# A hybrid diffusion step on one core: score products over all array rows, keys and queries in one transfer each

## The chip, the core and the metric

The kernel runs on one core of a Trainium2 chip. The core has a matrix engine (TensorE, PE in the rows; its weight loads are PEld), a vector engine (DVE), an activation engine (ACT), a general engine (POOL) and a queue engine that issues transfers (SP). Transfers between main memory and the on-chip memory run on 16 DMA engines that the core owns. The on-chip memory has 128 partitions. Each engine works through its own instruction list in order and waits on semaphores.

The metric is device time in microseconds (us) of one execution. Before the change three runs took 2118.08, 2121.22 and 2123.41 us, a median of 2121.22 us.

## The reference

One inference step for a context group (256 tokens) and a latent group (1024 tokens) that share their weights. Layer 0 mixes with attention and with an RWKV-7 scan side by side, layer 1 with gated linear attention (GLA). Cut to what matters here:

```python
def block_attention(q, k, v):                      # 8 query heads, 2 key/value heads, head size 64
    s = jnp.einsum('bqkgd,bskd->bkgqs', qi, k).astype(jnp.float32) * scale
    p = jax.nn.softmax(s, axis=-1)
    return jnp.einsum('bkgqs,bskd->bqkgd', p, v)

def even_mixer(h, ...):                            # layer 0
    qa, ka, va, ga, zb, gb = split_cols(h @ w_in, EV_SPLITS)
    q, k, v = rms_norm(qa), rms_norm(ka), va       # latent: rotary on q and k, cached keys in front
    o_a = block_attention(q, keys, vals) * silu(ga)
    zb = token_shift(zb, shift_mu)
    # RWKV-7, forward and backward: s = s*w + (s@-kk)(kk*a) + v k ; y = s@r
    o_b = (group_norm(y) + bonus) * silu(gb)
    return concatenate([o_a, o_b]) @ w_out

m = silu(cond) @ mod_w[i] + mod_b[i]               # shift, scale, gate of each layer
x = x + gate * mixer(rms_norm(x) * (1 + scale) + shift)
```

Latent queries attend to 512 cached, 1024 latent and no other keys; context queries to the 256 context keys.

## The kernel before, in words

**One list scheduler writes the order.** The kernel is written as many generators (tasks) that ask for buffers by a tag and record instructions. A class `Sched` holds a cost for each instruction (`_instr`), estimates when each engine is free and each buffer ready, and again and again issues the recorded instruction that could start first (`drive`). So the static order on every engine follows from these costs and from conditions between tasks (`sch.until`). All instructions are recorded by one helper, so nearly all rows of the profile name its line, L354 (L356 after the change). Groups are told apart by the names of their tiles. Compute instructions keep the scheduler's order. Transfers, all on SP's queue, keep their own order, which the framework makes and in which a transfer can stand earlier.

**Layer 0.** Tokens lie on the free axis (groups of 256, 512 and 512 tokens), channels on the partitions. Projections split numbers into a high and a low part (`hhi`, `hlo`, `whi`, `wlo`) and make three products. First come RWKV's inputs, the queries, keys and values and the eight gate units (`gated_unit`; the last ones write `gb`). Queries and keys are written to main memory as a high and a low part (`qh`, `kh`).

**The change of rooms.** When the layer's units are issued (`flags["left"] == 0`), `room_attn` closes the right half of the on-chip memory and opens attention's tiles there. When the eighth gate unit is over and `room_attn` is done, `room_rwkv` closes the left half (`hhi`, `hlo`, the weights) and opens RWKV's tiles, with masks to load and constants to fill (`LL`, `Z`, `ring`, `UV`, mostly on POOL and ACT). Then three kinds of work run side by side until about 1310 us: 40 RWKV segments (`rwkv_seg`, tiles `AR`, `BK`, `Vs`), twelve attention units, and the modulation products of the later layers (`mods`).

**Scores.** For each key/value head v the tile `KA[v]` holds the high parts of 64 channels in partitions 0 to 63 and the low parts in 64 to 127; `KB[v]` holds the high parts again and a row of ones in partition 64. For a query head `QA` holds the queries' high parts twice, and `QB` their low parts and in row 64 the negated maxima. `maxima` makes approximate scores with one product over `QA` and `KA` and reduces them on DVE (tile `mx`); the negated maxima (`mr`) go to `QB`'s row 64 by a small transfer. `attend` then makes the exact scores in two products, and ACT takes the exponential:

```python
PE.matmul(p[:, 0:n], lhsT=KA[kv][:, kc], rhs=Q[hh][0][:, 0:n], start=True, stop=False)
PE.matmul(p[:, 0:n], lhsT=KB[kv][0:65, kc], rhs=Q[hh][1][0:65, 0:n], start=False, stop=True)
```

There are 208 such pairs. `KA[v]` is filled by two transfers of 64 partitions, `QA` by two, `KB[v]` and `QB` by one each. There are four buffers of `QA` and of `QB`, so the queries of the next units are loaded while earlier ones are used.

**Modulation.** `mod_cols` loads 1 MB of `mod_w` into a buffer `mw` (in this stage there is one, so a load waits until the products of the one before have read it) and makes eight products that use 32 columns of the array each.

Of the kernel before, what the change touches and what calls it, by code (L numbers as in the profile page):

```python
# [22 lines left out]
NK = DM // P  # L23
# [80 lines left out]
class Sched:  # L104
# [71 lines left out]
    def _instr(self, name, op, f, a, k):  # L176
# [19 lines left out]
        if name == "pe":  # L196
            lhs = pattern(k.get("lhsT", a[1] if len(a) > 1 else None))
            m = 1
            for d in lhs.shape[1:]:
                m *= d  # L200
            rows = lhs.shape[0]
            turned = op == "transpose" or k.get("is_transpose")

            if turned:
                cost = max(2 * n / 2300, m / 1170)
            elif lhs.dtype == F32:
                cost = 2 * max(2 * n / 2300, m / 1170)
            elif lhs.dtype == F32R:
                cost = max(n / 2300, m / 1170)
            else:  # L210
                cost = max(n, 64) / 2300
            cost = 1.06 * cost + 0.0025
            size = lambda x: 32 if x <= 32 else 64 if x <= 64 else P
            late = (size(rows), size(m), lhs.start_partition() // 32, out.start_partition() // 32)
        elif name == "dve":
            srcs = [x for _, x in aps if x is not out]
            psum = any(x.tensor.space == PSUM for x in [out] + srcs)
            if op == "reduce_max":
                n = 1
                for d in srcs[0].shape[1:]:  # L220
                    n *= d
            wide = n
            if not psum and (op in ("tensor_copy", "tensor_scalar") or all(x.dtype == F16 for x in [out] + srcs)):
                wide = n / 2
            cost = (62 if psum else 66) / 960 + wide / 960
            if op == "reciprocal":
                cost = (62 + n * 6) / 960
            if op == "tensor_tensor_scan":
                cost += n / 960
            if out.shape[0] <= 64 and not n == 1:  # L230
                cost += 0.11
            late = not psum and op != "reduce_max"
            if op in ("tensor_scalar", "scalar_tensor_tensor"):
                cost += (0.0, 0.057, 0.09)[sum(1 for x in srcs if x.shape[1:] == [1] or tuple(x.shape[1:]) == (1,))] if n > 1 else 0.0
        elif name == "act":
            psum = any(x.tensor.space == PSUM for _, x in aps)
            cost = (0.051 if psum else 0.094) + n * 0.833e-3
            if n > 1:
                cost += (0.0, 0.05, 0.17)[min(2, sum(1 for q, x in aps if q in ("scale", "bias", 2)))]
            if out.shape[0] <= 64 and n > 1:  # L240
                cost += 0.11
        elif name == "pool":
            if op == "tensor_tensor":
                cost = 0.15 + n * (1.66e-3 if any(0 == d[0] for _, x in aps for d in x.ap[1:]) else 2.1e-3)
                if k.get("op", a[-1]) == ALU.pow:
                    cost = 0.56
            elif op == "memset":
                cost = 0.14 + n * 0.42e-3
            else:
                cost = 0.16 + n * (0.833e-3 if len(aps) == 2 else 1.5e-3)  # L250
            late = op != "memset"
        else:
            cost, late = 0.47, n * out.shape[0] * 4 / 270e3
        return f, a, k, name, cost, late, reads, writes, slots

    def _choice(self, slot, taken=()):
# [227 lines left out]
def tile_hybrid_dit_step(ctx: ExitStack, tc: tile.TileContext, I, C, O):  # L484
# [63 lines left out]
    def mod_cols(i, c0, n, bank, row, ready=lambda: True):  # L548
# [15 lines left out]
                b = yield from get(row, False)  # L564
                D.dma_start(out=b[0:2, 0:n], in_=I["mod_b"][i:i + 1, c0:c0 + n].to_broadcast([2, n]))
        yield from sch.until(ready)
        for a in range(2):
            with sch.together():
                for s in range(4):
                    k = 4 * a + s  # L570
                    PE.matmul(p[32 * s:32 * s + 32, :], lhsT=sT[:, k, :], rhs=ws[k // nk][:, k % nk, :], start=(a == 0), stop=(a == 1))
            for x in ws[4 * a // nk:4 * (a + 1) // nk]:
                put("mw", x)
        m4 = yield from get("m4", False)
        m = m4[:, 0:n]
        copy(m, p)
# [123 lines left out]
    vt_d = [dram.tile([T, P], F32, name=f"vt{p}") for p in range(4)]  # L700
    bv_d = [dram.tile([P, T], F32, name=f"bv{p}") for p in range(4)]
    kh_d = dram.tile([P, 2, PAST + T], F32, name="kh")
    vo_d = dram.tile([P, 14, P], F32, name="vo")
    ga_d = [dram.tile([P, T], F32, name=f"ga{p}") for p in range(4)]
    gb_d = [dram.tile([P, T], F32, name=f"gb{p}") for p in range(4)]
# [7 lines left out]
    get, put = sch.get, sch.put  # L713
    el = cst.tile([P, 2, 4, 20], F32, name="el")
    left, right = (ctx.enter_context(ExitStack()) for i in range(2))
    flags = dict(left=0, gates=0, attn=False, keys=False, rwkv=False, mods=False, normed=False, gla=False, gl=False, units=0)

    def pool(stack, name, **k):
        return stack.enter_context(tc.tile_pool(name=name, bufs=1, reuse_waits="tile", **k))
# [18 lines left out]
    def layer0():  # L738
# [44 lines left out]

        def gated(col, dst):

            def use(g, t0, n, p):
                t1 = yield from get("gt", False)
                S.activation(out=t1[:, 0:n], in_=p, func=AF.Tanh, scale=0.5)
                V.scalar_tensor_tensor(out=t1[:, 0:n], in0=t1[:, 0:n], scalar=1.0, in1=p, op0=ALU.add, op1=ALU.mult)
# [8 lines left out]
        def gated_unit(i, col, dst):  # L798
            yield from sch.until(lambda: flags["left"] <= GATES[i])
            yield from gated(col, dst)  # L800

            def done():
                flags["gates"] += 1
            sch.then(done)

        def gates():
            for i in range(8):
# [379 lines left out]
    def room_attn():  # L1187
# [11 lines left out]
        sT = ac.tile([P, NK, 32], F32, name="sT1")  # L1199
        for x in ("QA", "QB"):  # L1200
            slots(x, 4, [P, 512], F32R)
        slots("mx", 2, [P, 4, 4])
        slots("mr", 1, [4, P], F32R)
        slots("rcp", 1, [P, 512])
# [3 lines left out]
        yield from move("a", "po", 1)  # L1208
        yield from move("a", "b", 3)
        yield from move("pj", "b", 2)  # L1210
        for x in range(2):
            load_keys(0, x)
        for v in range(2):
            V.memset(KB[v][64:65, :].bitcast(F32), 1.0)
        D.dma_start(out=sT.rearrange("p k c -> p (k c)"), in_=sT_d)
        V.memset(ones64, 1.0)

# [3 lines left out]

    def load_keys(v, x):

        D.dma_start(out=(KA, KA, KB)[x][v][64 * (x % 2):64 * (x % 2) + 64, :].bitcast(F32), in_=kh_d[64 * v:64 * v + 64, x % 2, :])

    def keys():

        yield from sch.until(lambda: flags["attn"])
        for v, x in ((0, 2), (1, 0), (1, 1), (1, 2)):
            load_keys(v, x)  # L1230
            if (v, x) == (0, 2):
                D.dma_start(out=VO.rearrange("p t v d -> p t (v d)"), in_=vo_d)

        def done():
            flags["keys"] = True
        sch.then(done)

    def mods():
# [376 lines left out]
    def maxima(i, p4, g):  # L1615


        yield from sch.until(lambda: flags["attn"] and (p4 < 2 or flags["keys"]))
        t0, n, k0, nk = span(g)
        before = sum(scores(x) for _, x in units[0:i])  # L1620
        kv = p4 // 2
# [3 lines left out]
        for hh, hs in enumerate(halves):  # L1625
            QA = yield from get("QA")
            QB = yield from get("QB")
            for x in range(2):
                D.dma_start(out=QA[64 * x:64 * x + 64, 0:n].bitcast(F32), in_=qh_d[p4][hs, 0, t0:t0 + n])
            D.dma_start(out=QB[0:64, 0:n].bitcast(F32), in_=qh_d[p4][hs, 1, t0:t0 + n])  # L1630
            mx = yield from get("mx")
            for j in range(n // P):
# [22 lines left out]
    def attend(i, p4, g):  # L1655
# [11 lines left out]
        for kt in range(nk + 1):  # L1667
            new = []
            for hh in range(2):
                if kt < nk:  # L1670
# [5 lines left out]
                    p = yield from get("b", False)  # L1676
                    with sch.together():
                        PE.matmul(p[:, 0:n], lhsT=KA[kv][:, kc], rhs=Q[hh][0][:, 0:n], start=True, stop=False)
                        PE.matmul(p[:, 0:n], lhsT=KB[kv][0:65, kc], rhs=Q[hh][1][0:65, 0:n], start=False, stop=True)
                    S.activation(out=pt[:, 0:n], in_=p[:, 0:n], func=AF.Exp, scale=0.125)  # L1680
                    put("b", p)
                    new.append(pt)
# [704 lines left out]
```

## Time and profile before

| | |
|---|---|
| median of the runs | 2121.22 us |
| the profiled execution | 2118.56 us |
| its span, first to last instruction | 2116.8 us |
| PE busy | 1997.0 us (94%) |
| DVE, ACT, POOL busy | 69%, 48%, 15% |
| DMA | 217.10 MB on SP's queue, 32.6% of the 16 engines |
| mean granted clock of TensorE | 0.980 |

How to read it: the page divides the span by engine, and other views of the same trace give busy time by stretch, the list of instructions in order of time, the chain that ended last and the transfers with their sizes. An engine's busy time counts a matmul from its start to its modelled end, and matmuls overlap, so PE can be busy nearly all the time and still have room.

The stretch from 515 to 555 us is the change of rooms; in it PE waits more than anywhere else after the first 100 us. SP's instructions have the suffix q: their duration is that of issuing, not of moving the data.

### The profile page before, as it was taken

The page shows a single profiled execution, that of the slowest core. Times are in us where ns is not written, and L with a number is a line of the kernel's source. Part 1 is how long each engine was busy: PE and PEld are TensorE (multiplying, and loading weights), DVE is VectorE, ACT ScalarE, POOL GpSimd, SP SyncE. Part 2 cuts the span into 40 slices and gives each one's busy share as a digit, 9 for nine tenths or more (in the row PEclk, how much of TensorE's full clock was granted, in tenths as well). Part 3 has the DMA queues.
Part 4 walks back from the last instruction along what each step waited for, and adds up shares of the span by engine and source line. Part 5 has one row for each costly group of instructions (what it writes and reads, how often), then busy time and mean ns, then how long its engine had stood idle before and what let it go on. Part 6 is the DMA issues. An engine that isn't in the chain of part 4 may idle for free.

```text
span 2116.8 us, 38599 instructions
## 1 busy us (share of the span) xinstructions
PE 1997.0 (94%) x14876; PEld 1556.8 (74%) x14876; DVE 1456.1 (69%) x2852; ACT 1010.9 (48%) x2196; POOL 324.2 (15%) x392
## 2 busy tenths in 40 slices
PE   5999989999799999999999998999999999999998
PEld 3787777786477777777777754777777777778886
DVE  4578776767787888879887876643565656564455
ACT  4355554552466666665666543342445454542111
POOL 2011211102311111121112012110121212110011
PEclk7999999999899999999999999999999999999999
DMA  8234353526612241233222224442111111105653
GB/s 284 70 100 157 105 177 103 176 80 217 189 50 76 76 128 59 86 93 102 68 89 85 71 75 145 152 134 73 34 33 43 34 43 33 43 26 162 192 168 115
DMA packets 218264, 219.57 MB, mean 104 GB/s; under 512 B 20624, under 2 KB 164352, under 8 KB 218080
## 3 DMA queue, kind: packets, MB, share of 16 engines
q1 hardware_dynamic: 218080, 217.10, 32.6%
q8 instruction: 117, 1.92, 0.4%
q14 instruction: 67, 0.55, 0.1%
HBM read 149.63 MB, written 67.39 MB: 103 GB/s over the span
## 4 chain that ended last, share of the span: by engine, by line
PE 55%; DVE 11%; issue 3%; ACT 3%; DMA 2%; POOL 1%; SPq 0%; POOLq 0%; DVEq 0%; ACTq 0%
PE pj L354 28%; PE a L354 27%; DVE QQ L354 2%; DVE mx L354 1%; DVE dec L354 1%; ACT QQ L354 1%; DVE LL L354 1%; DVE gt L354 1%; DMA gb<-gt 1%; DMA x<-xt 1%; DVE acc L354 1%; DVE TT L354 1%; DVE Z L354 1%; POOL wol L354 0%; DMA wst<-o 0%
## 5 line engine op out<-in xcount | busy, mean ns | idle before, releaser
L354 PE MATMUL pj<-hhi,whi 128*128 128x512 f32 (+1 forms) x672 | 240.8, 360 | 5.6 <-DVE whi L354 2.9
L354 PE MATMUL pj<-hlo,whi 128*128 128x512 f32 (+1 forms) x672 | 241.0, 360 | 1.0 <-DVE hlo L354 1.0
L354 PE MATMUL pj<-hhi,wlo 128*128 128x512 f32 (+1 forms) x672 | 239.4, 360 | 2.2 <-DVE wlo L354 2.2
L354 PEld LDWEIGHTS pj<-hhi,whi 128*128 128x128 f32 x672 | 128.4, 191 | 29.0 <-issue 6.3
L354 PEld LDWEIGHTS pj<-hlo,whi 128*128 128x128 f32 x672 | 128.4, 192 | 24.8 <-issue 5.6
L354 PEld LDWEIGHTS pj<-hhi,wlo 128*128 128x128 f32 x672 | 128.2, 191 | 24.9 <-issue 4.2
L354 POOL TENSOR_TENSOR acc<-acc,pt 128x512 f32<-128x512 f32 (+1 forms) x57 | 75.8, 1337 | 457.1 <-ACT pt L354 325.7
L354 PE MATMUL a<-h1hi,whi 128*128 128x512 f32 (+3 forms) x304 | 111.1, 368 | 1.7 <-ACT whi L354 1.7
L354 PE MATMUL a<-h1lo,whi 128*128 128x512 f32 (+3 forms) x304 | 110.9, 366 | 0.0
L354 PE MATMUL pj<-h1lo,whi 128*128 128x512 f32 (+2 forms) x296 | 109.5, 370 | 1.3 <-DVE h1lo L354 1.3
L354 PE MATMUL pj<-h1hi,whi 128*128 128x512 f32 (+2 forms) x296 | 110.0, 372 | 0.0
L354 PE MATMUL pj<-h1hi,wlo 128*128 128x512 f32 (+1 forms) x288 | 107.2, 372 | 0.0
L354 PE MATMUL a<-h1hi,wlo 128*128 128x512 f32 (+1 forms) x288 | 105.5, 366 | 0.0
L354 PE MATMUL a<-pt,VO 128*64 128x512 f32 (+1 forms) x368 | 96.6, 604 | 1.2 <-ACT pt L354 1.2
L354 DVE TENSOR_TENSOR acc<-acc,pt 128x512 f32<-128x512 f32 (+1 forms) x127 | 89.0, 724 | 11.1 <-ACT pt L354 8.7
L354 POOL TENSOR_SCALAR sq<-sq 128x1 f32<-128x1 f32 x70 | 18.7, 267 | 442.0 <-ACT gt L354 157.7
L354 DVE TENSOR_REDUCE mx<-pj 128x1 f32<-128x512 f32 (+1 forms) x122 | 78.4, 655 | 5.6 <-PE pj L354 5.6
L354 ACT ACTIVATE pt<-pj 128x512 f32<-128x512 f32 (+1 forms) x103 | 58.6, 592 | 26.3 <-PE pj L354 18.0
L354 DVE TENSOR_REDUCE mx<-a 128x1 f32<-128x512 f32 (+1 forms) x86 | 56.6, 669 | 14.9 <-PE a L354 14.9
L354 PE MATMUL pj<-woh,oh 128*128 128x512 f32 (+1 forms) x160 | 61.1, 382 | 5.0 <-DVE oh L354 5.0
L354 PEld LDWEIGHTS a<-h1hi,whi 128*128 128x128 f32 (+1 forms) x304 | 56.5, 186 | 11.1 <-ACT whi L354 1.9
L354 PEld LDWEIGHTS pj<-h1lo,whi 128*128 128x128 f32 (+1 forms) x296 | 56.3, 190 | 10.5 <-DVE h1lo L354 1.7
(505 smaller groups left out, 5519.2 us busy)
## 6 DMA issues: line engine op xcount, KB each, us to landing
mw<-in_mod_w SPq DMA_DIRECT2D x24, 1024.0 KB
ws<-wk SPq DMA_DIRECT2D x32, 512.0 KB
wst<-in_ev_w_in SPq DMA_DIRECT2D x26, 512.0 KB
wst<-in_od_w_in SPq DMA_DIRECT2D x24, 512.0 KB
AR<-ws SPq DMA_DIRECT2D x40, 256.0 KB
BK<-ws SPq DMA_DIRECT2D x40, 256.0 KB
wst<-o SPq DMA_DIRECT2D x14, 512.0 KB
Vs<-vt SPq DMA_DIRECT2D x80, 64.0 KB
```

The costliest lines, as they stand in the source:

```text
L354: r = f(*a, **k)
```

## The change

Five edits stand in one diff.

- The second score product takes all 128 rows of `KB` and `QB`; their partitions 64 to 127 are zeroed once on POOL (with the ones of row 64 written after it, before on DVE).
- `KA[v]` and `QA` are each filled by one transfer of 128 partitions. Its source is written by `twice`: an access pattern whose outermost step runs twice (high and low parts of the keys; the same queries twice) and whose second step runs over 64 rows.
- The keys of the second key/value head are loaded in a later step of `keys`, and the first attention needs one flag where it needed all.
- A gate unit counts as over when the products of its third token group are issued, not when its store is; `room_rwkv` depends on that count.
- `mod_cols` puts the eight products of a 256-column block in one group, and the scheduler's cost of a transfer into or out of at most 64 partitions is larger.

```diff
-            cost, late = 0.47, n * out.shape[0] * 4 / 270e3
+            parts = [x.shape[0] for _, x in aps if x.tensor.space != DRAM]
+            cost, late = 0.47, n * out.shape[0] * 4 / (270e3 if not parts or parts[0] > 64 else 180e3)
...
-        for a in range(2):
+        for ks in [range(NK)] if nk == NK else (range(4), range(4, NK)):
             with sch.together():
-                for s in range(4):
-                    k = 4 * a + s
-                    PE.matmul(p[32 * s:32 * s + 32, :], lhsT=sT[:, k, :], rhs=ws[k // nk][:, k % nk, :], start=(a == 0), stop=(a == 1))
+                for k in ks:
+                    PE.matmul(p[32 * (k % 4):32 * (k % 4) + 32, :], lhsT=sT[:, k, :], rhs=ws[k // nk][:, k % nk, :],
+                              start=(k < 4), stop=(k >= 4))
...
+    twice = lambda x, r, c, s: bass.AP(tensor=x.tensor, offset=x.offset, ap=[[s, 2], [x.ap[0][0], r], [1, c]])
...
+            def done():
+                flags["gates"] += 1
+
             def use(g, t0, n, p):
+                if g == 2:
+                    sch.then(done)
...
-        for x in range(2):
-            load_keys(0, x)
+        load_keys(0, 0)
         for v in range(2):
-            V.memset(KB[v][64:65, :].bitcast(F32), 1.0)
+            G.memset(KB[v][64:128, :].bitcast(F32), 0.0)
+            G.memset(KB[v][64:65, :].bitcast(F32), 1.0)
...
-        D.dma_start(out=(KA, KA, KB)[x][v][64 * (x % 2):64 * (x % 2) + 64, :].bitcast(F32), in_=kh_d[64 * v:64 * v + 64, x % 2, :])
+        src = kh_d[64 * v:64 * v + 64, 0, :]
+        if x == 0:
+            D.dma_start(out=KA[v].bitcast(F32), in_=twice(src, 64, PAST + T, PAST + T))
+        else:
+            D.dma_start(out=KB[v][0:64, :].bitcast(F32), in_=src)
...
-            for x in range(2):
-                D.dma_start(out=QA[64 * x:64 * x + 64, 0:n].bitcast(F32), in_=qh_d[p4][hs, 0, t0:t0 + n])
+            D.dma_start(out=QA[:, 0:n].bitcast(F32), in_=twice(qh_d[p4][hs, 0, t0:t0 + n], 64, n, 0))
...
-                        PE.matmul(p[:, 0:n], lhsT=KB[kv][0:65, kc], rhs=Q[hh][1][0:65, 0:n], start=False, stop=True)
+                        PE.matmul(p[:, 0:n], lhsT=KB[kv][:, kc], rhs=Q[hh][1][:, 0:n], start=False, stop=True)
```

Up to the first transfer of `KA` every engine's order is the same in both kernels. From there on it differs on all of them. Three places matter.

SP at the opening of attention's room, before (`KA_3798` and `KA_3799` are the tiles of the two key/value heads, `mw` a block of modulation weights):

```order
L354 DMA KA_3798<-kh 64x1792 x2
L354 DMA sT_3806<-sT_d 128x256
L354 DMA QA_3807<-qh_101 64x512 x2
L354 DMA QB_3811<-qh_101 64x512
L354 DMA KB_3800<-kh 64x1792
L354 DMA VO<-vo 128x1792
L354 DMA KA_3799<-kh 64x1792 x2
L354 DMA gb_100<-gt_133 128x256
L354 DMA KB_3801<-kh 64x1792
L354 DMA mw_3804<-in_mod_w 128x8x256
L354 DMA gt_132<-in_mod_b 2x256
L354 DMA QA_3808<-qh_101 64x512 x2
```

SP at the same place after the change:

```order
L356 DMA KA_3798<-kh 128x1x1792
L356 DMA sT_3806<-sT_d 128x256
L356 DMA QA_3807<-qh_101 128x1x512
L356 DMA QB_3811<-qh_101 64x512
L356 DMA KB_3800<-kh 64x1792
L356 DMA VO<-vo 128x1792
L356 DMA mw_3804<-in_mod_w 128x8x256
L356 DMA gb_100<-gt_133 128x256
L356 DMA gt_132<-in_mod_b 2x256
L356 DMA QA_3808<-qh_101 128x1x512
L356 DMA QB_3812<-qh_101 64x512
L356 DMA gmask<-in_k_gmask 128x256
```

Three transfers of the second head have left the place, the first weights block stands right behind `VO`, and RWKV's first mask stands ahead of the first small `mr` transfer.

SP some 40 us later, before, around the first load of attention's gate `ga`:

```order
L354 DMA QA_3810<-qh_101 64x512 x2
L354 DMA QB_3814<-qh_101 64x512
L354 DMA BK_3977<-ws_75 128x512
L354 DMA ga_3825<-ga_93 128x512
L354 DMA Vs_3979<-vt_83 64x2x128 x2
L354 DMA Vs_3980<-vt_83 64x2x128 x2
L354 DMA AR_3973<-ws_76 128x512
L354 DMA BK_3978<-ws_76 128x512
```

SP there after the change:

```order
L356 DMA QA_3810<-qh_101 128x1x512
L356 DMA QB_3814<-qh_101 64x512
L356 DMA BK_4000<-ws_75 128x512
L356 DMA ga_3825<-ga_93 128x512
L356 DMA KA_3799<-kh 128x1x1792
L356 DMA KB_3801<-kh 64x1792
L356 DMA Vs_4002<-vt_83 64x2x128 x2
L356 DMA Vs_4003<-vt_83 64x2x128 x2
L356 DMA AR_3996<-ws_76 128x512
L356 DMA BK_4001<-ws_76 128x512
```

The keys of the second head now stand directly ahead of the loads of RWKV's fourth segment (`Vs`, `AR`).

PE from the last maxima of the second head to RWKV's first product, before:

```order
L354 MATMUL a_146<-KA_3798,QA_3808 128x512
L354 MATMUL pj_142<-mw_3804,sT_3806 32x256 x8
L354 MATMUL pj_143<-ident,mx_3816 4x128
L354 MATMUL pj_141<-AR_3973,BK_3976 128x128
L354 MATMUL pj_140<-AR_3973,BK_3976 128x128
```

PE there after the change:

```order
L356 MATMUL a_146<-KA_3798,QA_3808 128x512
L356 MATMUL pj_142<-mw_3804,sT_3806 32x256 x8
L356 MATMUL pj_140<-ident,mx_3816 4x128
L356 MATMUL pj_142<-m_0_3805,msel 2x256
L356 MATMUL pj_143<-QA_3807,KA_3798 128x512
L356 MATMUL pj_143<-QB_3811,KB_3800 128x512
L356 MATMUL a_145<-mw_3804,sT_3806 32x256 x8
L356 MATMUL a_146<-AR_3996,BK_3999 128x128
```

A first pair of scores and the products of a third weights block (`a_145<-mw`) now stand ahead of RWKV's first product.

## Rows read from the trace of the kernel before

**Rows 1.** Table by stretch: us, busy per engine, granted clock, DMA share, GB/s.

```profile
500.00:600.00 100.00, 84.10 (x662) 60.66 (x661) 74.64 (x157) 40.06 (x95) 28.41 (x45) 0.91 0.64 185
```

**Rows 2.** The same table, stretches of 4 us at the change of rooms.

```profile
510.00:514.00 4.00, 3.60 (x28) 3.23 (x26) 3.95 (x8) 0.95 (x2) 0.00 (x0) 1.00 0.51 192
514.00:518.00 4.00, 3.82 (x17) 3.10 (x17) 3.25 (x3) 0.38 (x1) 0.00 (x0) 1.00 1.14 350
...
534.00:538.00 4.00, 0.37 (x1) 0.08 (x1) 0.69 (x1) 0.86 (x2) 1.39 (x3) 0.50 1.05 263
```

**Rows 3.** PE in order of time: start, us, instruction, idle before it and releaser.

```profile
526.01 0.47 PE L354 MATMUL a<-KA,QA 128*128 128x512 f32 x1 [0.54 <-DMA QA<-qh]
...
534.04 0.37 PE L354 MATMUL pj<-ident,mx 128*4 128x128 f32 x1 [2.69 <-DVE mx L354]
541.25 1.93 PE L354 MATMUL a<-mw,sT 128*32 128x256 f32 x16 [6.84 <-DMA gb<-gt]
...
549.82 1.07 PE L354 MATMUL pj<-mw,sT 128*32 128x256 f32 x16 [0.43 <-DVE mx L354]
...
553.51 2.08 PE L354 MATMUL pj<-AR,BK 64*128 64x128 f32 x16
...
589.89 0.37 PE L354 MATMUL pj<-AR,BK 64*128 64x128 f32 x1
```

**Rows 4.** SP's queue in order of time: start and us of issuing.

```profile
515.92 2.23 SPq L354 DMA_DIRECT2D KA<-kh  x2
...
518.84 1.08 SPq L354 DMA_DIRECT2D QA<-qh  x2
...
543.23 0.38 SPq L354 DMA_DIRECT2D mw<-in_mod_w  x1
...
557.20 1.73 SPq L354 DMA_DIRECT2D QA<-qh  x2
...
582.50 0.33 SPq L354 DMA_DIRECT2D AR<-ws  x1
```

**Rows 5.** Transfers: packets by size, the queue (packets, MB, share), issues by kind.

```profile
DMA packets 218264, 219.57 MB, mean 104 GB/s; under 512 B 20624, under 2 KB 164352, under 8 KB 218080
...
q1 hardware_dynamic: 218080, 217.10, 32.6%
...
mw<-in_mod_w SPq DMA_DIRECT2D x24, 1024.0 KB
...
QA<-qh SPq DMA_DIRECT2D x32, 128.0 KB
...
KA<-kh SPq DMA_DIRECT2D x4, 448.0 KB
...
QB<-mr SPq DMA_DIRECT2D x16, 2.0 KB
...
gt<-in_mod_b SPq DMA_DIRECT2D x8, 2.0 KB
...
gate<-m SPq DMA_DIRECT2D x8, 2.0 KB
...
QB<-mr SPq DMA_DIRECT2D x8, 1.0 KB
...
msel<-in_k_msel SPq DMA_DIRECT2D x1, 1.0 KB
```

**Rows 6.** PE in order of time within the exact scores.

```profile
560.00 0.48 PE L354 MATMUL pj<-QA,KA 128*128 128x512 f32 x1
560.32 0.40 PE L354 MATMUL pj<-QB,KB 65*128 65x512 f32 x1
560.55 0.40 PE L354 MATMUL a<-QA,KA 128*128 128x512 f32 x1
```

**Rows 7.** DVE and POOL in order of time: the fills at the change of rooms.

```profile
514.67 1.55 DVE L354 MEMSET KB<- 1x1792 f32 x1 [0.43 <-issue]
...
525.30 1.84 POOL L354 MEMSET UV<- 128x1024 f32 x2 [17.13 <-PE pj L354]
```

More of the change, by code (lines that the diff above doesn't have):

```diff
@@ L566, in mod_cols @@
         yield from sch.until(ready)
-        for a in range(2):
+        for ks in [range(NK)] if nk == NK else (range(4), range(4, NK)):
             with sch.together():
-                for s in range(4):
-                    k = 4 * a + s
-                    PE.matmul(p[32 * s:32 * s + 32, :], lhsT=sT[:, k, :], rhs=ws[k // nk][:, k % nk, :], start=(a == 0), stop=(a == 1))
-            for x in ws[4 * a // nk:4 * (a + 1) // nk]:
-                put("mw", x)
+                for k in ks:
+                    PE.matmul(p[32 * (k % 4):32 * (k % 4) + 32, :], lhsT=sT[:, k, :], rhs=ws[k // nk][:, k % nk, :],
+                              start=(k < 4), stop=(k >= 4))
+            put("mw", ws[ks[0] // nk])
         m4 = yield from get("m4", False)
@@ L715, in tile_hybrid_dit_step @@
     left, right = (ctx.enter_context(ExitStack()) for i in range(2))
-    flags = dict(left=0, gates=0, attn=False, keys=False, rwkv=False, mods=False, normed=False, gla=False, gl=False, units=0)
+    flags = dict(left=0, gates=0, attn=False, keys=0, rwkv=False, mods=False, normed=False, gla=False, gl=False, units=0)
     def pool(stack, name, **k):
@@ L800, in gated_unit @@
             yield from gated(col, dst)
-            def done():
-                flags["gates"] += 1
-            sch.then(done)
         def gates():
@@ L1201, in room_attn @@
             slots(x, 4, [P, 512], F32R)
+        for x in [t.bitcast(F32) for t in sch.slot["QB"]]:
+            G.memset(x[64:128], 0.0)
         slots("mx", 2, [P, 4, 4])
@@ L1222, in load_keys @@
     def load_keys(v, x):
-        D.dma_start(out=(KA, KA, KB)[x][v][64 * (x % 2):64 * (x % 2) + 64, :].bitcast(F32), in_=kh_d[64 * v:64 * v + 64, x % 2, :])
+        src = kh_d[64 * v:64 * v + 64, 0, :]
[3 more added lines that the diff above has]
+            D.dma_start(out=KB[v][0:64, :].bitcast(F32), in_=src)
     def keys():
         yield from sch.until(lambda: flags["attn"])
[L1229 to L1232, printed above, removed]
         def done():
-            flags["keys"] = True
+            flags["keys"] += 1
+        load_keys(0, 1)
+        D.dma_start(out=VO.rearrange("p t v d -> p t (v d)"), in_=vo_d)
+        sch.then(done)
+        yield from sch.until(lambda: attended[1] >= 2)
+        for x in range(2):
+            load_keys(1, x)
         sch.then(done)
@@ L1615, in maxima @@
     def maxima(i, p4, g):
-        yield from sch.until(lambda: flags["attn"] and (p4 < 2 or flags["keys"]))
+        yield from sch.until(lambda: flags["attn"] and (p4 < 2 or flags["keys"] == 2))
         t0, n, k0, nk = span(g)
```

## Prediction

> **What bounds the kernel now.** Read the page's list of engines first: PE is busy 94% of the span, no other engine above 69%. Then the table by stretch: in 500 to 600 us, where one stage gives way to the next, PE is busy only 84% [rows 1]. All that the change moves lies behind 515 us, so that stretch comes next, in steps of 4 us [rows 2]: from 514 us the transfers fill all 16 DMA engines (share 1.14 at 350 GB/s, still 1.05 at 263 GB/s in 534 to 538), while PE does 0.37 of 4 us there and its granted clock falls from 1.00 (2.4 GHz) to 0.50 (1.2 GHz). PE's list says what it waits for [rows 3]: the first score product at 526.01 was released by the transfer of QA, the twelve maxima of the first head run to 534.04, and 6.84 us pass before the first modulation products at 541.25, which need a 1 MB block that came in behind the keys. (The row names a store of gb; the products read mw.) RWKV's first product stands at 553.51. So the opening is bound by transfers, and what follows, until about 1310 us, by PE in its fixed order.
>
> **How fast one DMA engine is, and how many a transfer gets.** The queue moved 217.10 MB in 32.6% of the time of 16 engines [rows 5]: 217.10 MB / (0.326 x 16 x 2116.8 us) = 19.7 kB/us for one engine. The stretches give 192/(16 x 0.51) = 23.5 at half load and 263/(16 x 1.05) = 15.7 when full [rows 2]. I take 19.7 and keep 15.7 and 23.5 as ends.
>
> The number of engines can be read from the small packets. The page counts 20,624 packets under 512 B [rows 5]. The code's shapes account for 8,640 of them as data rows (2,176 of 64 B, 6,144 of 256 B, 320 others); 11,984 are left. The list of issues has 782 transfers (103 rows; the first and the last are in [rows 5]). One closing packet for each engine and transfer would make 782 x 16 = 12,512, which is 528 too many. The list has 24 transfers whose outermost step runs twice (8 of mod_b, 8 of gate rows, 8 of mr with 1 KB) and 16 of mr where it runs four times [rows 5]. If these use 2 and 4 engines, 24 x 14 + 16 x 12 = 528 are missing: exactly the difference. So a transfer with an outermost step of two used two engines here. The trace shows it for small ones only. After the change the source of KA and of QA has such a step (`twice`), and I take it that they use two engines too.
>
> The Trainium skill (DMA: Bandwidth & Descriptors, "Why a DMA increments its semaphore by 16 and not by 1") says the number is the largest up to 16 that divides the slowest dimension of both sides, whatever the size; its "Rules for kernel authors" warn of an outermost broadcast of few copies. The count above agrees. The same list advises one 128-partition transfer in place of two halves; by that alone the edit would gain, which is the second rival below.
>
> **The change part by part.**
>
> *First keys and queries.* KA is 2 x 448 KB and QA 2 x 128 KB [rows 5], that is 459 and 131 kB for each of two engines: 23.3 us (19.5 to 29.2) and 6.7 us (5.6 to 8.3). KA is issued at 515.92 as before [rows 4]; the engines are full then, so I start it at 517. It ends at 540.3, QA behind it on the same engines at 547.0, and with 1 us to be seen PE begins at 548, not 526.01: 22 us late. PE's list has nothing else ahead of it, so nothing covers this. The twelve maxima take 8.0 us as before [rows 3]: 556. Behind the first QA the two engines bring their sixteenths of QB, KB, VO and the first weights block (160 kB, 8.1 us), then the second QA (6.7 us): 561.8, seen at 563. Twelve more maxima: 571. Then the new order of PE decides: products of the second block (1 us), a score pair, and the products of a third block, whose load can be issued only when the second has been read. From such an issue (543.23 [rows 4]) to its products (549.82 [rows 3]) took 6.6 us: 578.6, and 1.9 us of products. RWKV begins at 580 where it began at 553.51, 26.5 us late, with 2.4 us of work done that came later before. Term: **+24 us**; with the ends of the rate +17 and +36.
>
> *Second keys.* They leave the opening and stand directly ahead of the loads of RWKV's fourth segment. Ahead of them on the same two engines are two QA and a block. From the first of those (557.20 [rows 4], now 583): 6.7 + 3.3 + 6.7 + 23.3 + 1.5 for KB = 41.5 us, so the segment's AR comes at about 626. Before, it was issued at 582.50 [rows 4] and used at 589.89 [rows 3]; shifted by 26.5 it is wanted at 616. PE's order is fixed and stalls. Term: **+10 us** (0 to 20 with the ends of the rate).
>
> *The other 20 queries.* Each holds two engines for 6.7 us, and every transfer issued behind it needs these two for its sixteenth. A segment's loads come every 750/40 = 18.9 us at two moments, with 7.4 us from issue to use in the case above. Part of these the load itself takes; I leave 4 us of slack. A single query then delays what is issued within 2.7 us behind it, by 1.35 us on average: 20 x 2.7 x 2/18.9 x 1.35 = 8 us. If they come in pairs with 9.4 us beyond the slack: 10 x 9.4 x 2/18.9 x 4.7 = 47 us. If all have slack: 0. I take **+8 us**, since the order spreads many of the pairs.
>
> *Edits near nothing.* The product of 65 rows starts 0.32 us behind a first product of 128, and the next follows 0.23 us later [rows 6], the pace of full ones; 128 rows gain 0 to 208 x 0.01 = 2 us, and the granted clock in the stage is 1.00 already. I take 0. The two fills of KB leave DVE (1.55 us each [rows 7]), which then idles until the first maxima, so nothing is won. POOL gets four fills of 512 and four of 1792 columns; two of 1024 took 1.84 us [rows 7], so about 8.5 us, within the 17.13 us that POOL idled there. If they began late, the loads of KB and QB would wait on SP by as much; I take 0 (0 to 3). The grouping in mod_cols joins 12 pairs of groups; a product that follows another kind takes 0.48 us for 0.40 [rows 6], so 0 to 1 us is gained. RWKV's room opens some microseconds earlier, but its first product waits behind the third block on PE: 0 here. The new transfer cost moves the order of everything behind 515 us by some places: 0, with 5 us either way.
>
> Sum: 24 + 10 + 8 = 42 us on the profiled execution's 2118.56 us gives 2160.6. The runs' median lies 2.7 us above that execution: **2163 us**.
>
> **The rivals.**
>
> *The pairs collide* (slower still). The order puts up to four query loads within seven transfers; if RWKV's loads mostly fall behind them, 24 + 10 + 47 = 81 us: 2202. For it: no slack is known beyond the one case. Against: four buffers let the scheduler load queries far ahead of need, in quiet times.
>
> *Spread over 16 engines, and the opening gets shorter* (faster). If the large transfers are cut over all engines, the opening loses 3 x 448 KB of second keys; at 263 GB/s [rows 2] the first block comes 5.2 us sooner, at 536, PE's wait of 6.84 us [rows 3] shrinks to 1.6, and if the third block is loaded under the second maxima, all of it stays: 2121.2 - 5.2 = 2116. It decides from one point: whether KA is in before 525 us. For it: the full engines [rows 2]. Against: the 528 packets.
>
> *The same, but given back* (no change). The third block's 6.6 us stand ahead of RWKV's first product and take what the opening won: 2121, with 6 us either way by the new order.
>
> **How the numbers follow.** Two engines as summed 0.68, colliding pairs 0.10, spread and shorter 0.12, given back 0.10. About 0.3% (6.4 us) is what a measurement of this kernel can tell from no change. Faster by more: the third case with part of the last, 0.15; within: 0.05; slower: the first two with a little of the last, 0.80. The likeliest case by itself runs from 2138 (only the fast end of the first term) to 2192. To leave out no more than 2 in 10 the range goes from 2117 to 2198, down to the case of no change and up almost to the colliding pairs.
>
> **What would show it.** Right: PE's first score product near 548 us, released by QA, PE idle from 525 with the clock at 0.50; the DMA share in 525 to 545 us near 2/16 instead of 1; RWKV's first product near 580; a PE stall of about 10 us near 620 that ends with AR or Vs; the packets under 512 B fewer by 780 (52 transfers with 16 closing packets each go, 26 with two come; with 16 engines for the new ones it would be 416). The steps behind 1310 us keep their lengths. Wrong: a first score product at 526 and a full share in 518 to 530 would mean 16 engines, and all three terms fall. If RWKV begins near 580 and the end is still less than 20 us late, the later loads have more slack than I gave them.

## The result, and the profile after

The changed kernel takes 2184.72 us (median of 4 runs, 2181.57 to 2189.46) against 2121.27 us before (4 runs, 2118.08 to 2123.41). The ratio is 1.0302, 95% interval 1.0279 to 1.0325: slower by 63 us. The forecast was 2163 us, with a range of 2117 to 2198.

The profiled execution took 2189.46 us, 70.9 more than that of before. PE's list in order of time cuts this into parts. The marks are the last product of the gates (operand hhi), RWKV's first product (AR,BK), the last product with VO, and the first product of layer 1 (h1hi).

| us | before | after | difference |
|---|---|---|---|
| start to last gate product | 525.1 | 529.2 | +4.1 |
| to RWKV's first product ("opening") | 28.4 | 51.7 | +23.3 |
| to the last product with VO ("stage") | 758.2 | 795.6 | +37.4 |
| to layer 1's first product | 103.6 | 105.6 | +2.0 |
| layer 1 to the end | 701.5 | 705.5 | +4.0 |

The first line holds nothing that the change touches; what the last two hold it only puts in another order. This execution lies 4.7 us above its kernel's median and that of before 2.7 us below its own, and the 10.1 us of these three lines are taken, for the most part, as that.

The transfers first: the page's packet line and the queue (packets, MB, share of 16 engines), as in [rows 5].

```profile
DMA packets 217484, 219.57 MB, mean 100 GB/s; under 512 B 19844, under 2 KB 163572, under 8 KB 217300
...
q1 hardware_dynamic: 217300, 217.10, 31.5%
```

The packets under 512 B fell from 20,624 to 19,844, by 780: the number for two engines to each new transfer. The same bytes move, by fewer engines. The table by stretch shows it in time (columns as in [rows 1]):

```profile
526.00:530.00 4.00, 3.63 (x17) 2.66 (x15) 0.00 (x0) 0.00 (x0) 0.47 (x1) 1.00 0.13 54
530.00:534.00 4.00, 0.00 (x0) 0.00 (x0) 0.00 (x0) 0.00 (x0) 4.00 (x6) 0.75 0.13 54
534.00:538.00 4.00, 0.00 (x0) 0.00 (x0) 0.00 (x0) 0.00 (x0) 4.00 (x8) 0.50 0.13 54
538.00:542.00 4.00, 0.00 (x0) 0.00 (x0) 0.00 (x0) 0.00 (x0) 1.60 (x4) 0.50 0.77 169
...
546.00:550.00 4.00, 0.00 (x0) 0.00 (x0) 0.00 (x0) 0.00 (x0) 0.00 (x0) 0.50 1.09 271
```

A share of 0.13 is 2/16, at 54 GB/s. Before, the share at this place, from 522 to 538 us, was 1.00 to 1.11; one row of it:

```profile
530.00:534.00 4.00, 1.16 (x3) 0.37 (x2) 3.95 (x8) 0.00 (x0) 4.00 (x8) 0.87 1.02 240
```

After the change PE stands still and its granted clock goes to 0.50 (1.2 GHz). The full share comes only behind 538 us. SP's queue says why (start, us of issuing):

```profile
520.01 0.64 SPq L356 DMA_DIRECT2D KA<-kh  x1
520.71 0.74 SPq L356 DMA_DIRECT2D sT<-sT_d  x1
521.49 0.53 SPq L356 DMA_DIRECT2D QA<-qh  x1
522.12 16.14 SPq L356 DMA_DIRECT2D QB<-qh  x1
538.36 0.54 SPq L356 DMA_DIRECT2D KB<-kh  x1
```

With two transfers on two engines ahead of it, the issue of QB takes 16.14 us, and KB, VO and the weights stand behind it. It ends 18.3 us after KA was issued; KA's 0.92 MB at 54 GB/s are 17.0 us. So fourteen engines are idle for most of the time in which the queue is held. PE in order of time, to be read beside [rows 3]:

```profile
550.72 0.76 PE L356 MATMUL a<-KA,QA 128*128 128x512 f32 x1 [21.08 <-DMA QA<-qh]
...
559.24 1.91 PE L356 MATMUL a<-mw,sT 128*32 128x256 f32 x16
563.76 1.22 PE L356 MATMUL a<-KA,QA 128*128 128x512 f32 x2 [2.61 <-DMA QA<-qh]
...
580.91 1.44 PE L356 MATMUL a<-AR,BK 64*128 64x128 f32 x10
```

The first score product comes 21.5 us after the last gate product (before: 0.9), RWKV's first product at 580.91 instead of 553.51.

The second loss lies in the stage. One row of the table by stretch for it, before:

```profile
553.50:1311.70 758.20, 736.01 (x7563) 538.36 (x7562) 626.54 (x1367) 455.41 (x1105) 130.01 (x118) 0.99 0.29 88
```

and after:

```profile
581.00:1377.00 796.00, 745.05 (x7540) 544.73 (x7540) 624.73 (x1353) 450.96 (x1084) 151.03 (x142) 0.97 0.28 83
```

PE is idle for 51.0 us instead of 22.2, and busy 9.0 longer at a clock of 0.97 instead of 0.99. What PE waited for in the stage after (us in total, times, longest):

```profile
PE a L356 <- ACT UV L356: 9.8, 1, 9.8
PE pj L356 <- ACT UV L356: 5.8, 1, 5.8
PE a L356 <- DMA mw<-in_mod_w: 5.1, 1, 5.1
PE a L356 <- DMA QA<-qh: 5.0, 2, 3.7
PE a L356 <- DMA QB<-mr: 4.6, 1, 4.6
```

Only one of the five names a load of queries (`QA<-qh`). The 9.8 us come from a small transfer that stands behind query loads on SP's queue, as the third run below (E3) shows, and the 5.8 us stand behind the second keys (see the part on the prediction). The 5.1 and 4.6 us were not followed back; in E1 the same two waits are 2.1 and 1.8 us.

### The profile page after: what moved, and what is told of

It is laid out like the page before. It is cut to its first block, busy times and chain, and to the rows that moved or that the text cites. A ratio compares the mean times of both kernels' runs of the same rounds, so it can differ in the third digit from the quotient of the medians.

```text
span 2187.6 us, 38595 instructions
## 1 busy us (share of the span) xinstructions
PE 2021.7 (92%) x14876; PEld 1573.6 (72%) x14876; DVE 1456.2 (67%) x2848; ACT 1006.6 (46%) x2175; POOL 350.9 (16%) x423
## 2 busy tenths in 40 slices
DMA packets 217484, 219.57 MB, mean 100 GB/s; under 512 B 19844, under 2 KB 163572, under 8 KB 217300
## 3 DMA queue, kind: packets, MB, share of 16 engines
q8 instruction: 117, 1.92, 0.4%
## 5 line engine op out<-in xcount | busy, mean ns | idle before, releaser
L356 POOL TENSOR_TENSOR acc<-acc,pt 128x512 f32<-128x512 f32 (+1 forms) x75 | 96.4, 1294 | 445.8 <-ACT pt L356 286.0
L356 PE MATMUL a<-h1hi,whi 128*128 128x512 f32 (+2 forms) x304 | 111.9, 369 | 0.0
L356 PE MATMUL a<-h1lo,whi 128*128 128x512 f32 (+2 forms) x304 | 111.1, 367 | 0.0
L356 PE MATMUL a<-h1hi,wlo 128*128 128x512 f32 (+1 forms) x296 | 109.9, 371 | 0.0
L356 DVE TENSOR_REDUCE mx<-a 128x1 f32<-128x512 f32 (+1 forms) x97 | 62.9, 659 | 39.8 <-PE a L356 39.3
L356 DVE TENSOR_TENSOR acc<-acc,pt 128x512 f32<-128x512 f32 (+1 forms) x109 | 79.6, 751 | 11.2 <-ACT pt L356 8.3
L356 DVE TENSOR_REDUCE mx<-pj 128x1 f32<-128x512 f32 (+1 forms) x111 | 71.5, 662 | 4.1 <-PE pj L356 3.8
L356 PE MATMUL a<-KA,QA 128*128 128x512 f32 (+1 forms) x97 | 42.5, 475 | 29.0 <-DMA QA<-qh 28.7
L356 PEld LDWEIGHTS pj<-h1hi,whi 128*128 128x128 f32 (+1 forms) x296 | 56.7, 191 | 12.5 <-ACT whi L356 2.7
L356 PEld LDWEIGHTS <-TT 128*128 128x128 f16 x800 | 43.7, 100 | 29.0 <-DVE Z L356 9.3
```

The source lines that it names most:

```text
L356: r = f(*a, **k)
```

## The experiments

The theory: a transfer whose outermost step runs twice uses two DMA engines, and that is the whole loss. The rival: the other edits (order of second keys, modulation products and gates, planner's price, 128 rows) lose part of it. Times are medians beside runs of the kernel before on the same chip; ratios are to that kernel. "Opening" and "stage" are the two stretches of the table above, from each run's profiled execution.

| run | us | ratio, 95% interval | opening | stage |
|---|---|---|---|---|
| before | 2121.27 | 1 | 28.4 | 758.2 |
| after | 2184.72 | 1.0302 (1.0279 to 1.0325) | 51.7 | 795.6 |
| E1 rows outermost | 2125.12 | 1.0006 (0.9995 to 1.0017) | 26.8 | 762.4 |
| E2 keys on two | 2150.53 | 1.0125 (1.0107 to 1.0143) | 47.0 | 760.1 |
| E3 queries on two | 2163.91 | 1.0183 (1.0164 to 1.0201) | 38.2 | 786.7 |
| E5 before, two engines | 2179.53 | 1.0265 (1.0243 to 1.0287) | 68.9 | 776.4 |
| E6 E1 with 65 rows | 2128.95 | 1.0025 (1.0009 to 1.0040) | 28.4 | 762.4 |
| E7 before, sixteen engines | 2116.51 | 0.9967 (0.9955 to 0.9980) | 30.6 | 749.9 |
| E8 E1, spare transfers | 2167.31 | 1.0215 (1.0196 to 1.0234) | 27.6 | 763.1 |
| E14 E8, rows outermost | 2123.76 | 1.0006 (0.9993 to 1.0019) | 27.9 | 762.8 |
| E9 E1, gates as before | 2135.60 | 1.0064 (1.0043 to 1.0085) | 38.4 | 744.7 |
| E10 E1, one rate | 2118.56 | 0.9975 (0.9962 to 0.9989) | 27.0 | 746.1 |
| E12 E10, products in fours | 2113.53 | 0.9960 (0.9947 to 0.9974) | 26.6 | 746.7 |
| E15 E7 with the gates' edit | 2117.63 | 0.9978 (0.9965 to 0.9991) | 33.5 | 749.0 |

**E1.** One line differs from the changed kernel; the order of instructions stays.

```diff
-    twice = lambda x, r, c, s: bass.AP(tensor=x.tensor, offset=x.offset, ap=[[s, 2], [x.ap[0][0], r], [1, c]])
+    twice = lambda x, r, c, s: bass.AP(tensor=x.tensor, offset=x.offset, ap=[[x.ap[0][0], r], [s, 2], [1, c]])
```

> The changed kernel with one thing altered: the whole-partition transfers of keys and queries take their source with the 64 rows outermost and the pair (high and low part, or the same row twice) inside, so that the outermost count is 64 instead of 2 and both operands of the product have their partitions in the same new order. Instructions, bytes and their order stay. Theory A (a transfer whose outermost count is 2 runs on two DMA engines, and that is the whole loss): all of the +63 us goes, 2121 us, between 2112 and 2130; the first score product comes at most 3 us later after the last gate product than before, and no DMA share near 2/16 is left ahead of it. Rival B (the other edits lose the time: the new order of second keys, modulation products and gates, 128 rows): stays at 2185 us, or at least above 2150.

Measured 1.0006: the loss is gone, to within the interval. The packet line and PE in order of time:

```profile
DMA packets 217848, 219.57 MB, mean 103 GB/s; under 512 B 20208, under 2 KB 163936, under 8 KB 217664
```

```profile
528.11 0.47 PE L356 MATMUL a<-KA,QA 128*128 128x512 f32 x1
...
554.46 1.16 PE L356 MATMUL a<-AR,BK 64*128 64x128 f32 x16
```

416 small packets fewer than before, the count for sixteen engines (26 transfers fewer, each with 16 closing packets), and the first score product 0.4 us behind the last gate product. PE, DVE, ACT and POOL have the same list of instructions as in the changed kernel. Theory A holds; rival B falls as an account of the loss. What the other edits do to each other inside E1's zero is another question (E9, E10).

**E2 and E3.** The keys or the queries go back to two transfers of 64 partitions.

```diff
-            D.dma_start(out=QA[:, 0:n].bitcast(F32), in_=twice(qh_d[p4][hs, 0, t0:t0 + n], 64, n, 0))
+            for x in range(2):
+                D.dma_start(out=QA[64 * x:64 * x + 64, 0:n].bitcast(F32), in_=qh_d[p4][hs, 0, t0:t0 + n])
```

```diff
-            D.dma_start(out=KA[v].bitcast(F32), in_=twice(src, 64, PAST + T, PAST + T))
+            for y in range(2):
+                D.dma_start(out=KA[v][64 * y:64 * y + 64, :].bitcast(F32), in_=kh_d[64 * v:64 * v + 64, y, :])
```

> The changed kernel with the queries loaded as before, in two transfers of 64 partitions each; the keys alone keep the whole-partition transfer with the outermost count of 2. Theory A (two engines for a pair): the first keys are 0.92 MB at the 54 GB/s that the changed kernel shows there, 17 us, so the first score product comes near 540 instead of 526 and RWKV opens 10 to 15 us late; the second keys add up to 17 us more; together +25 us against the kernel before, 2146 us (2133 to 2160). Rival B (the queries' stalls are the loss): 2121 to 2130. Rival C (the rest of the change): 2185.

> The changed kernel with the keys loaded as before, in two transfers of 64 partitions each; the queries alone keep the whole-partition transfer with the outermost count of 2. Theory A (two engines for a pair): a query tile of 262 KB takes 4.9 us at 54 GB/s, the four of the opening cost a few us, and each of the other 20 up to 5 us where PE waits for it; together +25 us against the kernel before, 2146 us (2130 to 2165), so that this and the run with the keys alone add up to about the +63 of the change. Rival B (keys are the loss): 2121 to 2130. Rival C (the rest of the change): 2185.

Keys +1.25%, queries +1.83%: together 3.08% against 3.02% for the change. They add up in time, but the two runs can't be read alike. E3 keeps the order of E1 and of the changed kernel on PE, DVE, ACT and POOL. E2 does not: the planner orders all four engines otherwise from the opening on. So the loss is best divided in steps of one order, from E1 over E3 to the changed kernel:

| us | opening | stage |
|---|---|---|
| queries on two (E3 less E1) | 11.4 | 24.3 |
| keys on two as well (changed kernel less E3) | 13.5 | 8.9 |
| both | 24.9 | 33.2 |

In E2's own order the keys cost 20.2 us in the opening (47.0 against E1's 26.8), and its stage is 2.3 us shorter than E1's; PE of E2:

```profile
544.41 0.77 PE L356 MATMUL a<-KA,QA 128*128 128x512 f32 x1 [17.77 <-DMA QA<-qh]
...
573.28 0.37 PE L356 MATMUL pj<-AR,BK 64*128 64x128 f32 x1
```

The wait of 17.77 us is named after QA, which came in two halves here; KA's 0.92 MB take 17.0 at 54 GB/s. The second keys are on two engines too in E2, but since its order is another, its stage does not tell what they cost in the changed kernel; by the table above they cost 8.9 us there. The longest wait in E3's stage, in four views. SP's queue:

```profile
1241.64 0.53 SPq L356 DMA_DIRECT2D QA<-qh  x1
...
1242.83 0.53 SPq L356 DMA_DIRECT2D QA<-qh  x1
1243.45 2.32 SPq L356 DMA_DIRECT2D QB<-qh  x1
...
1247.10 5.14 SPq L356 DMA_DIRECT2D o<-ga  x1
1252.33 0.26 SPq L356 DMA_DIRECT2D gate<-m  x1
```

ACT:

```profile
1259.27 0.37 ACT L356 COPY m<-pj 128x256 f32<-128x256 f32 x1 [11.29 <-DMA gate<-m]
1259.54 1.18 ACT L356 COPY UV<-pj 64x512 f32<-64x512 f32 x2
```

PE:

```profile
1260.17 1.18 PE L356 MATMUL a<-GR,UV 128*128 128x128 f32 x3 [9.25 <-ACT UV L356]
```

And the same place of E1, SP's queue:

```profile
1220.93 0.53 SPq L356 DMA_DIRECT2D QA<-qh  x1
...
1224.73 0.53 SPq L356 DMA_DIRECT2D o<-ga  x1
1225.36 0.26 SPq L356 DMA_DIRECT2D gate<-m  x1
```

Two query loads; behind them SP is held, so a tiny transfer (gate, 2 KB) is issued 10.7 us after the first of them, in E1 4.4. ACT waits 11.29 us for it in its fixed order, 4.4 of them before the issue and the rest until it has landed; the copy of UV stands behind that on ACT; PE waits 9.25 us for UV. Nobody in this chain waits for a query. The first row of the changed kernel's list of waits, 9.8 us, is this same place. Elsewhere in E3's stage late queries do count, though for less; two rows of PE's list of waits there, which E1's list does not have:

```profile
PE a L356 <- DMA QA<-qh: 4.3, 2, 3.5
PE pj L356 <- DMA QA<-qh: 1.3, 1, 1.3
```

**E8 and E14.** E1 with a spare transfer behind each of the 24 query loads, into a buffer in main memory that nothing reads: in E8 with the pair outermost, in E14 with the rows outermost. PE, DVE, ACT and POOL keep the order of E1; on SP two other transfers stand a place or more elsewhere. E14 has E8's order on every engine.

```diff
+    again = lambda x, n: bass.AP(tensor=x.tensor, offset=x.offset, ap=[[0, 2], [x.ap[0][0], 64], [1, n]])
...
+            D.dma_start(out=spare.pop()[:, 0:n], in_=again(qh_d[p4][hs, 0, t0:t0 + n], n))
```

```diff
-    again = lambda x, n: bass.AP(tensor=x.tensor, offset=x.offset, ap=[[0, 2], [x.ap[0][0], 64], [1, n]])
+    again = lambda x, n: bass.AP(tensor=x.tensor, offset=x.offset, ap=[[x.ap[0][0], 64], [0, 2], [1, n]])
```

> The kernel with the 64 rows outermost, and behind each of its 24 query loads one more transfer with the outermost count of 2 of the same source rows into a DRAM buffer that nothing reads. All instructions but these 24 stand in the same order on every engine. Theory A1 (what is lost with the queries is mostly that a transfer on two engines holds back what the queue issues behind it): 20 to 40 us slower than with the 64 rows outermost alone, 2145 to 2165 us, with long issue times on the SP queue behind the spare transfers. Theory A2 (what is lost is the late arrival of the query tiles themselves): at most 8 us slower, 2125 to 2133 us.

> The run with 24 spare transfers once more, with the 64 rows outermost in the spare transfers too: the same bytes, the same order on every engine, 16 DMA engines instead of two. The run before it was 42 us slower than the kernel with the 64 rows outermost, all of it ahead of the first score product, where the spare transfers in fact ran (their rows were ready there). Theory A1 (the two engines hold back the queue): at most 8 us slower than the kernel with the 64 rows outermost, 2125 to 2133 us. Rival B (24 more transfers of 262 KB cost the time, however they are spread): again about 2167 us.

The spare transfers did not run where the queries do: the scheduler issued them as soon as their rows were ready, in layer 0's projections, and E8's whole loss (42 us more than E1 by the medians) lies ahead of 569 us, where E1 has 528. So the test stands at a place without query tiles, and the 20 to 40 us that were expected for the stage can't be compared with it. E8 in 300 to 325 us, SP:

```profile
301.54 9.99 SPq L358 DMA_DIRECT2D spare<-qh  x3
311.58 3.34 SPq L358 DMA_DIRECT2D rp<-in_k_cos  x1
321.64 0.33 SPq L358 DMA_DIRECT2D rp<-in_k_sin  x1
```

DVE's list of waits there (us in total, times, longest):

```profile
DVE qr L358 <- DMA rp<-in_k_cos: 8.7, 1, 8.7
```

PE there, and then the table by stretch:

```profile
324.19 0.58 PE L358 MATMUL pj<-hhi,wlo 128*128 128x256 f32 x1 [7.33 <-DVE wlo L358]
```

```profile
308.00:312.00 4.00, 4.00 (x19) 3.31 (x18) 1.16 (x3) 3.03 (x5) 0.00 (x0) 1.00 0.14 49
```

Three spare issues hold the queue for 9.99 us at a share of 0.14; the rotation tables (rp) behind them are late, DVE waits 8.7 us for one in its fixed order, and PE stops for 7.33 until DVE has made wlo. In 300 to 324 us PE is busy 16.36 us in E8 and 24.00 in E14. E14 moves the same bytes in the same order over sixteen engines and is 1.0006, equal to E1. So not the bytes, nor late queries, but two engines under one in-order queue make E8's loss. For the change itself this shows that such a transfer costs without a reader; how much of the 63 us comes that way, and how much from tiles that are late for their own reader, as in the opening, it does not say.

**E5 and E7.** The kernel before with the whole-partition transfers alone, pair outermost (E5) and rows outermost (E7).

> The kernel before with one part of the change alone: keys and queries by whole-partition transfers with the outermost count of 2, at the places where the two halves were issued. Order of the gates, modulation products, second keys and the 65 rows stay as they were. Theory A (two engines are the whole loss, wherever they stand): +55 to +75 us against the kernel before, about 2185 us, the first score product 16 to 24 us after the last gate product, and the stage from the first RWKV product to the last product with VO 20 us or more longer. Rival B (half of the loss comes from what the other edits do with these transfers): +20 to +45 us.

> The kernel before with whole-partition transfers of keys and queries alone, the 64 rows outermost, at the places where the two halves were issued. Theory A (with 16 engines a whole-partition transfer is worth about as much as its two halves, which lay behind other work): within 6 us of the kernel before, 2123 us (2117 to 2129). Rival B (28 transfers fewer on the queue gain): 6 us or more faster. Rival C: 6 us or more slower, by an order of products that the planner's other issue costs give.

E5 is 1.0265: most of the loss needs nothing but this part. Its opening is 68.9 us (both KA stand there), its stage 776.4, that is 18.2 longer than before where 20 or more was expected. E7 has E5's order on every engine, so these two make a clean pair: two engines cost 38.3 us in the opening and 26.5 in the stage. In the changed kernel, against E1, it is 24.9 and 33.2. That fits the second keys' leaving the opening, with less lost there and more behind it; but the other edits lie between the pairs too, so it is not shown to be the keys. E7 is 0.9967, a little faster than before. Both E5 and E7 differ from before in the order of every compute engine from the opening on, so whether the fewer transfers or the order gains is not shown. E7's stage is 8.3 us shorter than before; which waits went was not followed up.

**E6, E9, E10, E12, E15.** Single edits on sixteen engines. E6 uses rows 0:65 again and drops the zeros; E9 counts the last gate at the end of its unit; E10 has the planner's one rate:

```diff
-            cost, late = 0.47, n * out.shape[0] * 4 / (270e3 if not parts or parts[0] > 64 else 180e3)
+            cost, late = 0.47, n * out.shape[0] * 4 / 270e3
```

E12 is E10 with the modulation products in two groups of four; E15 is E7 with the gates' edit.

> The kernel with the 64 rows outermost (first run of this call), with the second product of the scores back on 65 array rows and without the zeros in the rows 65 to 127 of its operands. Theory A (the rows of the product cost and gain nothing, since its time goes by its columns): the same time as the first run of this call within 4 us, about 2121 us. Rival B (the full rows speed something up, a steadier clock among it): 5 us or more slower than that run. Rival C (zeros are a cost): 5 us or more faster.

> The kernel with the 64 rows outermost, with the last gate counted as before, when its unit is over, so that RWKV's room opens later. Theory A (the room's opening is worth nothing, since the first RWKV products wait for other things): within 5 us of the kernel with the 64 rows outermost, about 2124 us. Rival B (the earlier opening gains and the rest of the change costs as much): 5 to 12 us slower than that kernel. Rival C (it costs): 5 us or more faster.

> The kernel with the 64 rows outermost, with the planner's one rate for all transfers as before (270 KB per us), which moves products among each other on PE. Theory A (the planner's price moves the order and no time): within 5 us of the kernel with the 64 rows outermost, about 2124 us. Rival B (the new price is worth something): 5 us or more slower. Rival C (it costs): 5 us or more faster.

> The kernel with the 64 rows outermost and one planner's rate (0.9975 of the kernel before), with the products of the modulation columns in two groups of four as before. Theory A (the parts of the change that are left, gates and 128 rows, make its gain; the one group of eight makes none): within 5 us of that kernel, 2118 us. Rival B (eight in a row hold up the chain of RWKV behind them): 5 us or more faster, about 2112. Rival C (they gain): 5 us or more slower.

> The kernel before with two things alone: whole-partition transfers of keys and queries with the 64 rows outermost (0.9967 of the kernel before by themselves), and RWKV's room opened with the last gate's products. 65 rows, modulation products, second keys and planner as before. Theory A (the two add up: the run with the gates put back was 9 us slower than its neighbour): 2108 to 2115 us, ratio 0.993 to 0.996, the first RWKV product at most 28 us after the last gate product. Rival B (the opening is bound by the keys' scores by now and the gates are worth nothing): 2115 to 2120 us. Rival C (the other order costs): above 2120.

E6: 0.19% (4 us) slower than E1, and the intervals overlap; no effect of the rows is shown. E9: 0.58% (12 us) slower than E1 (rival B, at its upper end), with RWKV's first product 38.4 us after the last gate product instead of 26.8; there the gates' edit is worth something. But E9's order is another on every engine: its stage is 17.7 us shorter than E1's and the stretch from the last product with VO to layer 1 is 13.3 longer, so the 12 us are not shown to be the opening's. E15: the same edit on the order of before gains nothing (0.9978 against 0.9967, rival B, and its opening is 33.5 against 30.6). Its worth depends on the order around it. E10: 0.31% (6.6 us) faster than E1 (rival C, intervals apart): the new price of narrow transfers costs. E10's stage is 16.3 us shorter than E1's, but the stretch from there to layer 1 is 6.0 longer, so the stage alone overstates it. E12: 0.9960 against 0.9975, not told apart.

E7, E10, E12 and E15 are faster than both kernels, by 0.2% to 0.4% against the kernel before. E12 has the lowest median, 2113.53 us, but E7 is not told apart from it, and E7's edit changes only the way the two kinds of tiles are loaded.

## Why the prediction was right, and where its sizes were off

*Two engines.* Right. The 780 small packets, the share of 0.13 and the idle PE at half clock came as written, and E1 turns the whole loss off.

*First keys and queries, +24.* Right in size: 23.3 us, or 24.9 against E1. The working had two errors that nearly cancel, so the close match is in part luck. One engine of a lone pair moves 54/2 = 27 kB/us, above the end of 23.5 that I had allowed, so KA needs 17.0 us for 23.3. But I let QB, KB, VO and the weights be issued as before and be served in QA's shadow. In fact the queue was held until 538.36, and then they shared the two engines with QA, so that QA was seen at 550.7.

*Second keys, +10.* Right in size: 8.9 us more stage in the changed kernel than in E3, which has the same order and its keys in halves. The stall that I placed near 620 and gave to AR or Vs is there in the changed kernel, at about half of its size; ACT in order of time:

```profile
624.09 0.83 ACT L356 COPY UV<-Vs 64x256 f32<-64x256 f32 x2 [6.24 <-DMA Vs<-vt]
```

and PE:

```profile
624.99 2.08 PE L356 MATMUL pj<-AR,BK 64*128 64x128 f32 x16 [5.76 <-ACT UV L356]
```

So PE stood 5.76 us for Vs by way of UV. E3 and E1 have no such wait at this place. The other 3.1 us of the 8.9 were not followed back, and each side is one execution. E2, with the same keys in another order, has a stall of 3.19 us for AR near 610 and no longer stage than E1: what this term costs depends on the order.

*The other 20 queries, +8.* Mis-sized: 24.3 us (E3 against E1, in one order). This is the term of the sum that was wrong. I counted the time by which a transfer behind a query is late for its own user, and averaged over slack. What is lost goes further: the late one holds the next issue on SP, a small transfer then holds ACT's fixed order, and a product on PE pays for both. What was measured lies between my 8 and the 47 us of the working for pairs. The longest wait does stand behind a pair; for the other places this was not followed up. Nor was every load as long as I took it: eight of the 24 are half the size, which by itself would have made the term smaller. The two later-load terms together: 18 forecast, 33 measured against E1 (37 against before, whose stage is 4 us shorter than E1's). That is 15 to 19 of the 22 us by which the forecast is low; this term alone is 16 of them.

*Edits near nothing, 0.* Their sum is 0 (E1: +0.06%), the parts are not: the gates' edit saves 12 us in this order (E9), the planner's price costs 6.6 (E10). I had 0 for the gates "behind the third block on PE" and 0 with 5 either way for the price. The rest of E1's sum was not taken apart.

*The rivals.* "Spread over 16 engines" is what E1 makes true by another order of steps. Its time is then 2125 us, which is the third rival's 2121 with 6 either way and not the second's 2116; its opening is 1.6 us shorter than before and its stage 4.2 longer. With two engines neither came about. The Trainium skill (DMA: Bandwidth & Descriptors, "Rules for kernel authors") advises one 128-partition transfer in place of two halves, and warns of an outermost broadcast of few copies. The warning is borne out here: E5 is 63 us slower than E7, which has the same transfers in the same order with the rows outermost. For the advice, E7 is 0.33% faster than the kernel before, but since the order of its instructions differs, no run here shows that the whole-partition transfer by itself gains.

## What to carry to other kernels

When a transfer gets a leading step of 2, count its engines before counting its bytes; the small packets and the DMA share (2/16) show it at once, and swapping the order of the steps on both sides of the product can cost nothing. A slow transfer on an in-order queue is paid by what is issued behind it, so price it by the chain behind the queue (the next small load, the engine that waits for it in order, the product behind that) as well as by who reads its data. An edit that moves a planner's order has no worth of its own: the gates' edit was worth 12 us in one order and nothing in another.

## What was not expected of the hardware

A DMA engine in a lone pair moved 27 kB/us (54 GB/s at a share of 0.13), more than the 23.5 at half load and the 15.7 at full load [rows 2]. And the issue itself is held: with two such transfers outstanding the next issue on SP took 16.14 us in the changed kernel and 16.01 in E5, until about 18.3 us after the first of them was issued. In E2, with one such transfer ahead, QB's issue took 1.92 us. What holds the issue is not shown by these traces.
